# A hybrid recurrence block: TensorE's instructions in the order of emission instead of the scheduler's, in the part with the recurrences

## The chip, the cores and the metric

One Trainium2 chip, one of its cores. The kernel is one program with one launch. The metric is the time of one execution on the device in microseconds (us), as a median over runs; lower is better. TensorE (PE in the rows) multiplies matrices out of on-chip memory into PSUM, VectorE (DVE), ScalarE (ACT) and GpSimd (POOL) do the elementwise work, and SyncE (SP) issues most transfers. Each engine takes its instructions strictly one after the other, and an instruction waits on semaphores until what it reads has been written.

## The reference, cut to what matters

One layer on 256 latent and 256 context tokens with 2048 channels. A modulated norm is followed by one wide projection; its columns feed two recurrent branches (RWKV-7 and a gated delta rule, each in two directions, the latent scan starting from the context's last state) and two merge gates. Then up-projections, gates, an output projection, a residual, and a squared-ReLU MLP with a second residual and a last norm.

```python
    p = h @ in_w
    pc = hc @ (in_w[:, :A_COLS + B_COLS] if last else in_w)
    ...
    ya, ya_c = rwkv7_branch(pa.astype(f32), pca.astype(f32), ...)
    yb, yb_c = gdn_branch(pb.astype(f32), pcb.astype(f32), ...)

    x = x + g1 * merge_branches(ya.astype(dt), yb.astype(dt), pg, up_a, up_b, out_w)
    x = x + g2 * squared_relu_mlp(modulate(rms_norm(x, norm2_w), sh2, sc2), mlp_w1, mlp_w2)
```

All is float32. A dense product is made of three matmuls on operands split into a high and a low part (`mm3`, lines 239 to 241), which run in the type float32r; the recurrences use plain float32 matmuls.

## The kernel before, in words

The time falls into four stretches. To about 180 us the modulation and the first projections are made. From there to about 1455 us runs the part with the recurrences, which this change is about. Then come the merge and the output projection (to about 1800 us) and the MLP.

In the part with the recurrences four kinds of work are woven together. The **dense** work is projections (`projg`): 16 steps over the k tiles, three matmuls a step, of 256 or 512 columns, into a PSUM tile `dacc` of which there are two. Three **lanes** run beside it, each a Python generator: `preps` prepares a pair of heads (eight pairs), `invs` inverts the triangular 32 x 32 blocks of a pair, and `chains` walks through the chunks of a pair. When the RWKV pairs are through, the same lanes do the gated delta rule (`gpreps`, `ginvs`, `gchains`), with the merge's gates and up-projections as dense work.

`weave` sets the order in which all of this is emitted. Every `yield` of the dense generator says how long TensorE is busy with the step; every `yield` of a lane says how much dense time is to pass before the lane's next step. So the distance between two dependent steps of a lane is written by hand, in units of dense work. Where a generator emits two dependent things with no `yield` between them, they are emitted side by side.

The order of emission isn't the order on the engines: a scheduler sorts each engine's instructions when the program is built. It takes emission order as a priority, but puts an instruction later where, by its own reckoning, its inputs are not there yet, and takes others in between. From then on each engine's order is fixed.

The places that the prediction speaks of:

- `l2n` and `conv_silu` (lines 590 to 610): a head's q or k columns are convolved, gated and normalised. After the last matmul of the projection come ScalarE (591), VectorE (595, 596), ScalarE (598), VectorE (599) and ScalarE (603); then TensorE multiplies the squares by a matrix of ones (604). No `yield` stands between. Eight of these have 256 columns (q), eight 512 (k). In `prep` (line 647) the same is done for RWKV's k, behind six operations of VectorE (437) and two of ScalarE (434, 646), eight times, seven of them in this part.
- `tri_inv` (lines 465 to 482): one VectorE transpose (469), then 31 times two dependent VectorE operations (478, 480), then a transpose back (481). TensorE's line 811 (RWKV) or 1146 (delta rule) reads the result. The blocks that are inverted come from TensorE's lines 741 and 744 (RWKV) or 1079 (delta rule). There are eight inversions for RWKV and four for the delta rule, and the lane lets dense work pass at nine places in each.
- `wgran` (line 217): a weight tile is brought in by SyncE and split by ScalarE (226) and VectorE (227), with the highest priority.
- `gemv_steps` (line 279): the modulation's rows, fp32 matmuls of 512 columns (289), now and then between dense steps; a copy of the sums (294), then small matmuls on the copy (300, 309).

Of the kernel before, what the change touches and what calls it, by code (L numbers as in the profile page):

```python
# [131 lines left out]
def body(tc, A, out, dbg=None):  # L132
# [33 lines left out]
    class First:  # L166
        """An engine whose instructions go ahead of the others that are ready."""
# [12 lines left out]
    def weave(dense, lanes):  # L180
        """Emits dense, whose steps say how long the tensor engine is at them, and between its steps those of the lanes, which
        say how long to let pass before the next one. lanes: (generator, stretch)."""
        t, at = 0.0, [[g, 0.0, f] for g, f in lanes]

        def step(a):
            try:
                a[1] = max(a[1], t - 1) + next(a[0]) * a[2]
            except StopIteration:
                at.remove(a)

        slot = 0
        for c in dense:
            t += c
            if t < slot:
                continue
            slot = t + Q
            for a in list(at):
                while a in at and a[1] <= t + Q / 2:
                    step(a)
        while at:  # L200
            for a in list(at):
                step(a)

    nraw, more = 0, None  # the room that a phase adds to the ring of weights: a pool's tag, and how many of its tiles
# [9 lines left out]
    def wgran(src):  # L214
        """Half a megabyte of weights [128, K, C]: for each half of K (hi, lo), in tiles of their own."""
        K, w = src.shape[1], src.shape[2]
        raw = rawt()
        nc.sync.dma_start(out=raw[:, :K * w].rearrange("p (k c) -> p k c", k=K), in_=src)
        F = K // 2 * w
        r = []  # L220
        for i in range(2):
            hi = stream.tile([128, 512], F32R, tag="hi", name="hi")
            lo = stream.tile([128, 512], F32R, tag="lo", name="lo")
            x = raw[:, i * F:(i + 1) * F]
            with tc.high_priority(1000000):
                S.copy(out=hi[:, :F], in_=x)  # L226
                V.tensor_tensor(out=lo[:, :F], in0=x, in1=hi[:, :F].bitcast(F32), op=ALU.subtract)  # L227
            r.append((hi, lo))
        return r

    def wk_(g, k, w):
        """The (hi, lo) columns of k tile k, w wide, out of a granule of eight (w = 128) or two (w = 512) k tiles."""
        n = 512 // 128 if w != 512 else 1
        hi, lo = g[k // n]
        c = slice(k % n * w, k % n * w + w)
        return hi[:, c], lo[:, c]
# [26 lines left out]
    # modulation per channel: columns (x, ctx) for chunk tiles  # L263
# [15 lines left out]
    def gemv_steps(n, pool, acc, ahead=0):  # L279
        """Row n of the modulation, one half-megabyte of weights a step; at last the sums as four groups of rows."""  # L280
# [35 lines left out]
    # the same room once the projections are through: yb (0:8), the merged halves (8:24), ya (24:32), then half the MLP  # L316
# [18 lines left out]
    with ExitStack() as st:  # L335
        p0 = st.enter_context(tc.tile_pool(name="p0", bufs=2, reuse_waits="tile"))
        psg = st.enter_context(tc.tile_pool(name="psg0", bufs=1, space=PSUM))
        # x / sqrt(mean(x^2) + eps)
# [16 lines left out]
        def part(j):  # L355
            """The projections of first over the k tiles 4 j to 4 j + 3."""
# [73 lines left out]
    # z' = z + (shift(z) - z) mu ; natural order [ctx | x]  # L430
# [21 lines left out]
    def fl(ap, d, n=512):  # L452
        """[P, n] in scan order of direction d."""
# [8 lines left out]
    def tri_inv(pool, dg, xt):  # L462
        """X = (I - L)^-1 of the strictly upper 32 x 32 blocks L = dg[32 q:32 q + 32, u, :32], sixteen in each group of 32
        partitions: blocks to lanes (two lanes a block, one for the even rows of X and one for the odd ones), then row by
        row of L. Writes X^T to xt, in the places of dg."""
# [18 lines left out]
    def gate(j, tile_):  # L484
        """tanh of half the gate columns j of the merge, to DRAM."""
# [19 lines left out]
    def dense(every, *gens):  # L505
        """The steps of gens, and after each so many of them one of the modulation's."""
# [9 lines left out]
    with ExitStack() as st:  # L516
# [12 lines left out]
        def decays():  # L529
            """The decay and beta of the delta rule, token-major [tok, tile, (dir, head)]."""  # L530
# [124 lines left out]
        def prep2(p, R):  # L655
            zk, zv, zr, kk = (R[n] for n in ("zk", "zv", "zr", "kk"))
            # lora weights of this pair
# [8 lines left out]
            for d in range(2):  # L666
                # decay
# [8 lines left out]
                # the products up to a token (inclusive) or before it (exclusive), in the direction's order  # L676
# [14 lines left out]
                # in-context rate  # L691
# [27 lines left out]
                # bonus  # L719
# [5 lines left out]
                # pairwise products inside a chunk  # L725
# [40 lines left out]
                # token-major beta, kappa  # L766
# [12 lines left out]
            # the bonus  # L779
# [7 lines left out]
        def inv2(p, R):  # L787
            """The inverses of the chunks: a comes before b."""
# [40 lines left out]
            # values by tokens, in the rows beside their head's state  # L829
# [10 lines left out]
        ORD = ((0, 1, 2, 3, 4, 5, 6, 7), (3, 2, 1, 0, 7, 6, 5, 4))  # the chunks in the order in which a direction goes through them  # L840
        VL = S1.copy

        def chain(p, R):
            vt = R["vt"]

            def vload(d, sgm):
                """[S | U] beside V for two chunks; head 0 has V in the upper rows, head 1 in the lower ones."""
# [74 lines left out]
            # readout  # L922
# [40 lines left out]
        def rgates():  # L963
            """The gates of RWKV for all pairs."""
# [51 lines left out]
        GL = []  # the decays; the masks of a tile's pairs  # L1016
# [9 lines left out]
        NAT = ((0, 1, 2, 3), (1, 0, 3, 2))  # the tiles in the order in which a direction goes through them  # L1026
# [6 lines left out]
        def ltile(h, d):  # L1033
            """Room for the pairwise products of a head and direction, for three heads in turn."""
# [11 lines left out]
        def gprep(hh, hi_, R):  # L1046
            """Both directions in the tokens' own order: what comes first lies above the diagonal or below it."""
# [61 lines left out]
        def ginv(R, begun, wait):  # L1109
            """The inverses of 128 tokens out of those of 32, both directions at once: r0 comes before r1."""  # L1110
# [163 lines left out]
        gated, spilt = [], []  # the heads of yb that were done before the last product out of hT  # L1274
# [25 lines left out]
        def room():  # L1300
            """What is left of the inverses' room goes to the ring of weights."""
# [25 lines left out]
        def works():  # L1327
            nonlocal every
            yield from work()
            every = 12  # L1330
            yield from gwork()

        mpool = gpp
        weave(dense(lambda: every, works()),
# [7 lines left out]
    with ExitStack() as st:  # L1342
# [44 lines left out]
        def gate2():  # L1387
            """The second gate, in every partition."""
# [20 lines left out]
        def tokmm(src, kts, acts, n, done):  # L1409
            """out[tok, 512 columns n] over k tiles kts; acts[k] the [k, tok] pair."""  # L1410
# [18 lines left out]
        def resid(i, n, ps, c):  # L1429
            """x += gate * ps for the columns n; with c, the sum of their squares to column c."""  # L1430
# [15 lines left out]
        # x1 by channels, scaled but for its norm; beside it the shift, whose product with w1 is added after the norm  # L1446
# [90 lines left out]
```

## Time and profile before

| | before |
|---|---|
| median of 3 runs | 2349.41 us (2346.86 to 2351.87) |
| profiled execution, first to last instruction | 2348.0 us |
| TensorE matmuls busy | 2252.8 us |
| TensorE weight loads busy | 1795.2 us |
| VectorE busy | 1584.3 us |
| ScalarE busy | 1349.2 us |

The profiled execution has no time of its own beside its span; the span lies 1.4 us under the median of the runs. Matmuls are pipelined and overlap in the records, so the busy time of TensorE has to be read together with how many matmuls start in a stretch.

### The profile page before, as it was taken

The numbers are of one execution on the slowest core, as the hardware profiler recorded it, in microseconds if no ns is written. First come the engines' busy times: TensorE is split into PE (matmuls) and PEld (weight loads), VectorE is DVE, ScalarE is ACT, GpSimd is POOL, SyncE is SP. The second block draws the span as 40 slices with busy tenths as digits, with TensorE's granted clock in tenths as the row PEclk, the third lists the DMA queues.
The fourth block names the chain that finished last, engine by engine and source line by source line (L and its number), as shares of the span: only waits on it lengthen the run. The fifth ranks groups of instructions, "written<-read, shape, count | busy, mean of one in ns | idle before, by whom it ended". The sixth has DMA issues, their size and how long they took to land.

```text
span 2348.0 us, 45265 instructions
## 1 busy us (share of the span) xinstructions
PE 2252.8 (96%) x16886; PEld 1795.2 (76%) x16886; DVE 1584.3 (67%) x3590; ACT 1349.2 (57%) x3003; POOL 158.4 (7%) x343
## 2 busy tenths in 40 slices
PE   6989999999999999999999999999999999999997
PEld 2557676766667676678787888878999888999886
DVE  2357885858686867668577786876887555666555
ACT  3235758475758575855565766456555444555544
POOL 0001021111111111111000000000000000000000
PEclk9999999999999999999999999999999999999999
DMA  9954333333333343457566554875776666555664
GB/s 363 311 166 136 109 109 103 131 106 120 108 118 118 120 125 108 147 174 234 180 215 217 188 159 138 292 255 181 251 259 216 194 192 196 181 181 182 193 193 149
DMA packets 184371, 417.94 MB, mean 178 GB/s; under 512 B 15380, under 2 KB 37076, under 8 KB 183128
## 3 DMA queue, kind: packets, MB, share of 16 engines
q1 hardware_dynamic: 183576, 414.02, 55.1%
q8 instruction: 132, 2.16, 0.4%
q10 hardware_dynamic: 576, 1.05, 0.1%
q14 instruction: 87, 0.71, 0.1%
HBM read 399.63 MB, written 15.38 MB: 177 GB/s over the span
## 4 chain that ended last, share of the span: by engine, by line
PE 65%; ACT 6%; DVE 3%; DMA 2%; issue 1%; SPq 0%; ACTq 0%; DVEq 0%
PE dacc L239 12%; PE dacc L241 11%; PE dacc L240 11%; PE dacc L1423 3%; PE pm L1422 3%; PE pm L1421 3%; PE pm L1423 3%; PE dacc L1422 3%; PE dacc L1421 3%; PE vacc L289 3%; ACT hi L226 1%; DMA raw<-in_mod_w_dram 1%; DVE lo L227 1%; DMA raw<-in_w_pg_dram 1%; PE cb L889 1%
## 5 line engine op out<-in xcount | busy, mean ns | idle before, releaser
L227 DVE TENSOR_TENSOR lo<-raw,hi 128x512 fp32r<-128x512 f32 (+1 forms) x1032 | 693.0, 677 | 456.4 <-ACT hi L226 272.7
L226 ACT CAST hi<-raw 128x512 fp32r<-128x512 f32 (+1 forms) x1032 | 625.7, 610 | 646.1 <-PE dacc L240 315.4
L239 PE MATMUL dacc<-hh,hi 128*128 128x256 f32 (+1 forms) x1648 | 562.4, 342 | 8.5 <-ACT hh L244 3.5
L241 PE MATMUL dacc<-hh,lo 128*128 128x256 f32 (+1 forms) x1648 | 531.0, 322 | 1.3 <-DVE lo L227 1.2
L240 PE MATMUL dacc<-hl,hi 128*128 128x256 f32 (+1 forms) x1648 | 530.5, 322 | 0.0
L239 PEld LDWEIGHTS dacc<-hh,hi 128*128 128x128 f32 x1648 | 313.8, 191 | 98.9 <-issue 56.0
L241 PEld LDWEIGHTS dacc<-hh,lo 128*128 128x128 f32 x1648 | 314.1, 191 | 26.2 <-issue 3.5
L240 PEld LDWEIGHTS dacc<-hl,hi 128*128 128x128 f32 x1648 | 314.8, 191 | 23.5 <-issue 7.0
L241 PE MATMUL dacc<-ah,lo 128*128 128x258 f32 x1024 | 291.7, 285 | 1.7 <-DVE lo L227 1.6
L239 PE MATMUL dacc<-ah,hi 128*128 128x258 f32 x1024 | 290.8, 284 | 1.1 <-ACT ah L244 1.1
L240 PE MATMUL dacc<-al,hi 128*128 128x258 f32 x1024 | 290.1, 283 | 0.0
L241 PEld LDWEIGHTS dacc<-ah,lo 128*128 128x128 f32 x1024 | 194.2, 190 | 4.1 <-DVE lo L227 3.0
L239 PEld LDWEIGHTS dacc<-ah,hi 128*128 128x128 f32 x1024 | 194.6, 190 | 2.4 <-ACT ah L244 1.3
L240 PEld LDWEIGHTS dacc<-al,hi 128*128 128x128 f32 x1024 | 194.3, 190 | 1.1 <-issue 1.0
L175 POOL TENSOR_SCALAR sp<-vu,pc 64x64 f32<-64x64 f32 x224 | 128.2, 572 | 408.9 <-DVE vu L175 357.0
L1423 PE MATMUL dacc<-lo,hh 128*128 128x512 f32 x320 | 125.8, 393 | 4.0 <-DVE lo L227 3.8
L1421 PE MATMUL dacc<-hi,hh 128*128 128x512 f32 x320 | 125.0, 391 | 0.3 <-ACT hi L226 0.3
L1421 PE MATMUL pm<-hi,hh 128*128 128x512 f32 x320 | 124.8, 390 | 0.0
L1422 PE MATMUL dacc<-hi,hl 128*128 128x512 f32 x320 | 124.8, 390 | 0.0
L1423 PE MATMUL pm<-lo,hh 128*128 128x512 f32 x320 | 124.6, 389 | 0.0
L1422 PE MATMUL pm<-hi,hl 128*128 128x512 f32 x320 | 124.6, 389 | 0.0
L289 PE MATMUL vacc<-raw,sc_st 128*32 128x512 f32 x384 | 113.5, 605 | 1.6 <-DMA raw<-in_mod_w_dram 1.6
(411 smaller groups left out, 3255.9 us busy)
## 6 DMA issues: line engine op xcount, KB each, us to landing
raw<-in_w_dram SPq DMA_DIRECT2D x256, 512.0 KB
raw<-in_mod_w_dram SPq DMA_DIRECT2D x192, 512.0 KB
raw<-in_w_gdn_dram SPq DMA_DIRECT2D x64, 512.0 KB
raw<-in_w_pg_dram SPq DMA_DIRECT2D x64, 512.0 KB
raw<-in_w_rkv_dram SPq DMA_DIRECT2D x40, 512.0 KB
raw<-in_out_w_dram SPq DMA_DIRECT2D x32, 512.0 KB
raw<-in_upa_dram SPq DMA_DIRECT2D x16, 512.0 KB
raw<-in_upb_dram SPq DMA_DIRECT2D x16, 512.0 KB
```

The source lines that it names most:

```text
L175: return getattr(self.eng, name)(*a, **k)
L226: S.copy(out=hi[:, :F], in_=x)
L227: V.tensor_tensor(out=lo[:, :F], in0=x, in1=hi[:, :F].bitcast(F32), op=ALU.subtract)
L239: P.matmul(out=o, lhsT=wh, rhs=ah, start=first, stop=False)
L240: P.matmul(out=o, lhsT=wh, rhs=al, start=False, stop=False)
L241: P.matmul(out=o, lhsT=wl, rhs=ah, start=False, stop=last)
L289: P.matmul(out=pm[32 * g:32 * g + 32, :], lhsT=sc_st[:, 2 * k:2 * k + 32], rhs=raw[:, r * 512:(r + 1) * 512], start=(k < 4), stop=(k >= 12 ...
L889: P.matmul(out=cbs[d][hr[h], 64:128], lhsT=R["ti"][hr[h], d * 8 + ns[d], :], rhs=rss[d][hr[h], :], start=True, stop=True)
L1421: P.matmul(out=pss[i], lhsT=ah[:, tsl], rhs=wh, start=first, stop=False)
L1422: P.matmul(out=pss[i], lhsT=al[:, tsl], rhs=wh, start=False, stop=False)
L1423: P.matmul(out=pss[i], lhsT=ah[:, tsl], rhs=wl, start=False, stop=last)
```

## The change

The call of `weave` for the part with the recurrences now stands inside a region that orders TensorE: there each TensorE instruction is issued in the order in which the kernel emits it. The order on the other engines, and where the region's instructions fall among those emitted outside it, stay the scheduler's. Nothing is added, removed or computed in another way; comments and descriptive strings were dropped, and lines behind the change carry a number higher by one.

```diff
         mpool = gpp
-        weave(dense(lambda: every, works()),
+        with tc.manual_schedule(engines={mybir.EngineType.PE}):
+            weave(dense(lambda: every, works()),
               [(both(chains(), stretch(F_GC / F_C, gchains())), F_C), (both(invs(), ginvs()), F_I),
                (both(preps(), stretch(F_GP / F_P, gpreps())), F_P)])
         for _ in md:
             pass
```

**First place: TensorE at the norm of a head's q** (second pair of heads). `dacc` is the PSUM tile of a projection, `hh` and `hl` are the split activations by k tile (hh_102 is the first k tile, hh_132 the last), `hi` and `lo` the split weights, `gth` the squares. Before, the row of line 604 stands in the middle of the next projection, which has 512 columns; its own projection, of 256 columns, ended 34 rows earlier:

```order
L239 MATMUL dacc<-hh_114,hi 128x512
L240 MATMUL dacc<-hl_115,hi 128x512
L241 MATMUL dacc<-hh_114,lo 128x512
L239 MATMUL dacc<-hh_116,hi 128x512
L240 MATMUL dacc<-hl_117,hi 128x512
L241 MATMUL dacc<-hh_116,lo 128x512
L239 MATMUL dacc<-hh_118,hi 128x512
L604 MATMUL dacc<-gth,cs 128x256
L240 MATMUL dacc<-hl_119,hi 128x512
```

In the changed kernel, TensorE at the same place:

```order
L239 MATMUL dacc<-hh_130,hi 128x256
L240 MATMUL dacc<-hl_131,hi 128x256
L241 MATMUL dacc<-hh_130,lo 128x256
L239 MATMUL dacc<-hh_132,hi 128x256
L240 MATMUL dacc<-hl_133,hi 128x256
L241 MATMUL dacc<-hh_132,lo 128x256
L604 MATMUL dacc<-gth,cs 128x256
L239 MATMUL dacc<-hh_102,hi 128x512
L240 MATMUL dacc<-hl_103,hi 128x512
```

Line 604 moved up to the row directly behind the last matmul of its own projection, and the whole next projection now stands behind it.

**Second place: TensorE at an inversion** (fifth pair of heads). `pr` is the PSUM tile of the inversion, `ti` and `X` hold the inverses that VectorE makes, `off` the other blocks; `cb` belongs to the chain of the pair before. Before, 90 dense matmuls of 256 columns and 69 of 512 stand between the last row of line 741 and the first of line 811, whose surroundings are:

```order
L912 MATMUL cb<-mb,vu 64x64 x2
L239 MATMUL dacc<-hh_110,hi 128x512
L240 MATMUL dacc<-hl_111,hi 128x512
L241 MATMUL dacc<-hh_110,lo 128x512
L239 MATMUL dacc<-hh_112,hi 128x512
L240 MATMUL dacc<-hl_113,hi 128x512
L241 MATMUL dacc<-hh_112,lo 128x512
L239 MATMUL dacc<-hh_114,hi 128x512
L240 MATMUL dacc<-hl_115,hi 128x512
L241 MATMUL dacc<-hh_114,lo 128x512
L811 MATMUL pr<-ti,off 32x32
L239 MATMUL dacc<-hh_116,hi 128x512
```

In the changed kernel 42 of 256 and 42 of 512 columns stand between them:

```order
L871 MATMUL cb<-vu,eb 64x64 x4
L239 MATMUL dacc<-hh_126,hi 128x512
L240 MATMUL dacc<-hl_127,hi 128x512
L241 MATMUL dacc<-hh_126,lo 128x512
L239 MATMUL dacc<-hh_128,hi 128x512
L240 MATMUL dacc<-hl_129,hi 128x512
L241 MATMUL dacc<-hh_128,lo 128x512
L811 MATMUL pr<-ti,off 32x32
L811 MATMUL pr<-X,off 32x32
L811 MATMUL pr<-ti,off 32x32
L811 MATMUL pr<-X,off 32x32
```

Line 811 moved up past 75 dense matmuls, and all 32 of its rows now stand together.

**Third place: VectorE inside the same inversion.** `Lt` and `ltmp` are the inversion's, `lo` a weight split, `vu` the chain's state, `zr` a projection's result. Before:

```order
L469 STREAM_TRANSPOSE Lt<-dg 128x32x32
L478 TENSOR_TENSOR ltmp<-X,Lt 128x31
L227 TENSOR_TENSOR lo<-raw,hi 128x512
L175 SCALAR_TENSOR_TENSOR vu<-cb,pc,sp 64x64 x4
L783 TENSOR_TENSOR bs<-pg,zv 128x256
L480 TENSOR_TENSOR X<-X,ltmp 128x31
L478 TENSOR_TENSOR ltmp<-X,Lt 128x30
L480 TENSOR_TENSOR X<-X,ltmp 128x30
L478 TENSOR_TENSOR ltmp<-X,Lt 128x58
L227 TENSOR_TENSOR lo<-raw,hi 128x512
```

In the changed kernel:

```order
L469 STREAM_TRANSPOSE Lt<-dg 128x32x32
L478 TENSOR_TENSOR ltmp<-X,Lt 128x31
L480 TENSOR_TENSOR X<-X,ltmp 128x31
L478 TENSOR_TENSOR ltmp<-X,Lt 128x30
L480 TENSOR_TENSOR X<-X,ltmp 128x30
L478 TENSOR_TENSOR ltmp<-X,Lt 128x58
L480 TENSOR_TENSOR X<-X,ltmp 128x2x29
L478 TENSOR_TENSOR ltmp<-X,Lt 128x56
L480 TENSOR_TENSOR X<-X,ltmp 128x2x28
L478 TENSOR_TENSOR ltmp<-X,Lt 128x81
```

VectorE's other instructions moved out of the beginning of the inversion. Between lines 469 and 481 of this inversion stand 38 other instructions before and 18 in the changed kernel.

## Rows read from the trace of the kernel before

**Rows 1.** The page's first line.

```profile
span 2348.0 us, 45265 instructions
```

**Rows 2.** Busy time of each engine by stretch: start:end, length, busy us (instructions), clock, DMA.

```profile
180.00:1455.00 1275.00, 1235.98 (x10740) 931.46 (x10739) 921.35 (x2379) 828.74 (x1987) 157.10 (x332) 0.99 0.46 143
2050.00:2100.00 50.00, 50.00 (x417) 50.00 (x416) 32.33 (x60) 28.17 (x61) 0.00 (x0) 1.00 0.58 186
1850.00:1900.00 50.00, 50.00 (x223) 41.39 (x222) 27.46 (x41) 23.38 (x38) 0.00 (x0) 1.00 0.63 194
```

**Rows 3.** TensorE's waits, 180 to 1455 us: total us, times, longest.

```profile
PE dacc L604 <- ACT gth L603: 5.3, 5, 2.7
PE pr L811 <- DVE ti L481: 3.6, 4, 1.2
```

**Rows 4.** Timeline of one norm of 256 columns: start us, us, engine, line.

```profile
365.36 0.46 ACT L591 ACTIVATE qv<-dacc,vs 128x256 f32<-128x256 f32 x1
...
366.27 0.48 DVE L595 SCALAR_TENSOR_TENSOR qv<-dacc,vs,qv 128x255 f32<-128x255 f32 x1
...
367.00 0.47 DVE L596 SCALAR_TENSOR_TENSOR qv<-dacc,vs,qv 128x255 f32<-128x255 f32 x1
...
367.57 0.42 ACT L598 ACTIVATE gth<-qv 128x256 f32<-128x256 f32 x1 [0.23 <-DVE qv L596]
...
369.22 0.42 DVE L599 SCALAR_TENSOR_TENSOR qv<-gth,qv 128x256 f32<-128x256 f32 x1
...
369.67 0.42 ACT L603 ACTIVATE gth<-qv 128x256 f32<-128x256 f32 x1
...
370.14 0.48 PE L604 MATMUL dacc<-gth,cs 128*128 128x256 f32 x1 [0.26 <-ACT gth L603]
```

**Rows 5.** Timeline of one norm of 512 columns, first and last step.

```profile
493.75 0.67 ACT L591 ACTIVATE kv<-dacc,vs 128x512 f32<-128x512 f32 x1
...
499.60 1.22 PE L604 MATMUL dacc<-gth,cs 128*128 128x512 f32 x1 [2.70 <-ACT gth L603]
```

**Rows 6.** VectorE's inversion groups, 180 to 1455 us: busy us, mean ns | idle before.

```profile
L478 DVE TENSOR_TENSOR ltmp<-X,Lt 128x126 f32<-128x126 f32 (+22 forms) x372 | 94.1, 253 | 7.3
L480 DVE TENSOR_TENSOR X<-X,ltmp 128x126 f32<-128x126 f32 (+22 forms) x372 | 93.9, 252 | 8.1
```

**Rows 7.** Timeline of the fifth inversion: its input, first and last steps, and reader.

```profile
652.44 1.16 PE L741 MATMUL pg<-eb,bk 64*128 64x128 f32 x16
...
659.42 1.99 DVE L469 STREAM_TRANSPOSE Lt<-dg 128x1024 f32<-128x1024 f32 x1
...
699.01 1.11 DVE L481 STREAM_TRANSPOSE ti<-X 128x512 f32<-128x512 f32 x1
...
700.54 0.24 PE L811 MATMUL pr<-ti,off 32*32 32x32 f32 x2
```

**Rows 8.** Groups of VectorE's other work, 180 to 1455 us.

```profile
L227 DVE TENSOR_TENSOR lo<-raw,hi 128x512 fp32r<-128x512 f32 x372 | 253.9, 688 | 150.5 <-ACT hi L226 131.0 <-PE dacc L239 5.3 <-PE dacc L241 4.3
...
L175 DVE SCALAR_TENSOR_TENSOR vu<-cb,pc,sp 64x64 f32<-64x64 f32 x224 | 59.9, 282 | 32.9 <-PE cb L905 19.7 <-PE cb L912 6.1 <-POOL vu L175 1.6
```

**Rows 9.** A small matmul and the copy of the modulation's sums, 180 to 1455 us.

```profile
L889 PE MATMUL cb<-rs,ti 64*64 64x64 f32 x512 | 30.6, 231 | 0.8 <-ACT rs L175 0.6
...
L294 ACT COPY rows<-vacc 128x512 f32<-128x512 f32 x12 | 7.1, 589 | 8.1 <-PE vacc L289 8.1
```

**Rows 10.** Busy time by stretch behind one stop of TensorE, and around another.

```profile
175.00:180.00 5.00, 5.00 (x20) 3.73 (x21) 2.70 (x8) 3.28 (x5) 0.00 (x0) 0.64 0.00 0
...
1380.00:1385.00 5.00, 1.92 (x12) 1.54 (x12) 4.64 (x13) 3.48 (x7) 0.00 (x0) 0.85 0.50 172
1385.00:1390.00 5.00, 4.38 (x20) 4.38 (x21) 3.73 (x13) 1.35 (x3) 0.00 (x0) 0.50 0.54 158
```

**Rows 11.** Timeline of TensorE where dense work follows a small matmul.

```profile
1350.30 0.36 PE L240 MATMUL dacc<-hl,hi 128*128 128x256 f32 x1
1350.50 0.28 PE L241 MATMUL dacc<-hh,lo 128*128 128x256 f32 x1
```

## The prediction

> **What bounds the kernel now.** I read the stretches first. The part with the recurrences takes 1275 us of the span of 2348.0 [rows 1, 2], and in it some TensorE matmul is open for 1236 us. The first thing to see is that nearly nothing else could end this stretch: VectorE is busy 921 us, ScalarE 829. The second is how fast dense work goes when nothing is in its way: in the MLP 417 matmuls of 258 columns start in 50 us, 0.120 us each, and 223 of 512 columns, 0.224 us each [rows 2]. These two prices I use for all dense work that covers a wait. The third is the list of TensorE's waits: its longest entries in this part are only 5.3 us (line 604) and 3.6 us (line 811) in total [rows 3]. So before the change the results that come back from VectorE and ScalarE are hidden almost wholly, and the question is what hides them in the new order.
>
> **What the change does, place by place.** It adds and removes nothing. It fixes where TensorE must stand still until a result arrives. In the order before, such rows stand late enough; in the new one each stands where it was emitted. For every row of TensorE that reads another engine's result I compare the work that TensorE has between the result's own source and that row (the cover) with the time that the result needs.
>
> Chain steps of RWKV (lines 871, 889, 905) keep what they had: the lane's yields leave some 2 to 5 us of TensorE's work between two steps in either order. They cost nothing new, and neither do lines 741 and 771, whose covers hardly change.
>
> *1. The norms, lines 604 and 647.* In the new order line 604 stands directly behind the last matmul of the projection that it normalises. What must happen in between is six dependent steps. For 256 columns they last 0.46 + 0.48 + 0.47 + 0.42 + 0.42 + 0.42 = 2.7 us, and in the instance shown 4.8 us passed from the first step to the matmul, since other work lay between them on both engines [rows 4]. I take the middle, 3.7 us: TensorE stands, so less new work arrives, but weight splits go first. For 512 columns the same took 5.85 us [rows 5]; a wider operation isn't faster, so 2.7 is the lower end, and I take 5.0, near the row. Line 647 has eight steps of 512 columns or half of it, and I give it 5.0 too. Eight of the first kind, seven of the second (the eighth lies inside an inversion), and four of line 647 (three others stand behind an inversion's stop, which hides them): 8 x 3.7 + 11 x 5.0 = 85 us (51 to 103).
>
> *2. RWKV's inversions, line 811.* The result needs 1.99 + 31 x (0.253 + 0.252) + 1.11 = 18.8 us of VectorE alone [rows 6, 7], and before it 5.8 us from the end of line 741 (652.44 + 1.16) to the start of line 469 [rows 7]. In the new order VectorE has 18 to 26 other instructions inside the inversion (11 in the first pair), 22 on the mean, from 0.282 to 0.688 us each [rows 8]; at 0.45 that is 10 us. Together 34.6 us. The cover in the new order of the fifth pair is 42 x 0.120 + 42 x 0.224 = 14.4 us of dense work; the mean over the second to the seventh pair is 13.4. To this come 40 chain matmuls at 0.12 us (30.6 us over 256, each of which has two records) [rows 9], 4.8 us, and some 20 others, for which I take 4.2. So 22.4 us, and a stop of 12.2 us, seven times. The first pair has only 10.8 + 4 us of cover against 29.6, 14.8 us. Sum 100 us. The bounds: with no other work on VectorE 24.6 − 22.4 = 2.2 us each and 9.8 for the first pair, 25 us in all; with VectorE as slow as before, when line 811 came 46.9 us behind line 741 [rows 7], 24.5 us each, 196 us. I stand between, since the new order of VectorE has about half as much other work inside an inversion, not none.
>
> *3. The delta rule's inversions, line 1146.* The four covers lose 264 matmuls of 256 columns together, 32 us at 0.120; VectorE's order has 42 fewer other instructions inside, 19 us at 0.45. The stop lies between 13 and 32 us in all; bounded below by 0 if the waits before were slack. I take 20.
>
> *4. Small stops.* The modulation's copies (589 ns, [rows 9]) stand directly ahead of their readers twelve times; some 20 further places (the second half of line 834, the one-time gates and decays, the first pair) are alike. 32 x 0.6 = 19 us (7 to 32).
>
> *5. What comes back.* Dense work and small matmuls alternate 1094 times in the old order and 936 times in the new one. A dense matmul of 256 columns behind a small one is followed after 0.20 us, not after 0.12 [rows 2, 11]; 158 x 0.08 = 13 us. The waits of [rows 3], 9 us, are part of the span and are replaced by the new ones. Minus 22 us.
>
> *6. The clock.* After a stop of some microseconds the rows show TensorE at its lower level, 1.2 GHz, for a part of the next stretch: a granted clock of 0.64 from 175 to 180 us, 1.8 us lost, and 0.50 from 1385 to 1390 us behind a stop, 2.5 us lost [rows 10]. The eleven long stops of points 2 and 3 at 2.2 us make 24 us (0 to 28). The Trainium skill's page "TensorE: Matmul & The Clock Gate" (section "HAM oscillation — how this bites in real kernels") tells of a kernel that fell back to the lower clock at each of its repeated waits; by that the short stops of point 1 would pay as well. No row here shows a stop of that length with its clock, so this is left to the upper rival.
>
> Sum: 85 + 100 + 20 + 19 − 22 + 24 = 226 us on the profiled 2348.0, so 2574; the median lies 1.4 us above the span, so I forecast **2575 us**, slower by some 9 to 10%. A change of 0.2% is about what a measurement of this kernel can tell from none.
>
> **The rivals.**
>
> *Only the norms stop.* VectorE, with TensorE standing still at the norms, may be ahead when an inversion begins, and point 2 falls to its lower bound, 25 us, point 3 to nothing, the clock to 5. For it: VectorE is idle for a good quarter of the stretch (921 of 1275 us [rows 2]). Against it: none of the norms stands inside the first seven inversions in the new order, and 18.8 us of dependent steps leave 3.6 us. 85 + 25 + 19 − 22 + 5 = 112 us: 2461.
>
> *VectorE stays as slow as before, and every stop costs clock.* Point 2 rises to 196 us, and the 19 short stops of point 1 pay the clock as the long ones do, 19 x 2.2 = 42 us: 226 + 96 + 42 = 364 us: 2713. For it: the weight splits (0.688 us [rows 8]) go ahead of everything. Against it: the third place of the new order, where ten rows of the inversion stand without a stranger.
>
> *Not slower: the emission order is good enough.* One mechanism: the hand-set distances cover the results, and what remains is point 5, minus 22 us: 2327. It decides where the cover exceeds the result's time; behind line 604 that cover is nothing. For it speaks that the chain's steps are covered in both orders, and that weight loads, another measure, are open for 931 of 1275 us only [rows 2]. The Trainium skill's page "Trainium Kernel Development and Optimization" (section "Performance Expectations") calls matmul busy time a bad metric and weight-load time a good one; by it a quarter of the stretch is slack. Against it: slack on TensorE is of use only where the order lets other work in, and the new order lets none in.
>
> **How the numbers follow.** My forecast 0.62; only the norms 0.16; the slow VectorE 0.17; not slower 0.05 (faster 0.04, the same 0.01). The forecast's own range is 2500 to 2650. To hold 8 in 10 the whole range goes to 2440 at the lower end (into the first rival) and 2700 at the upper (into the second): 0.05 and about half of each of the two lie outside, near 0.2. Chances: faster 0.04, the same 0.01, slower 0.95.
>
> **What would show it.** Point 1: line 604 waits for line 603 sixteen times, 3 to 6 us each, most of 90 us in the list of waits. Point 2: line 811 waits for line 481 eight times, about 12 us each. Point 3: line 1146 the same, about 5 us each. Point 5: the other waits of the stretch stay small, and the MLP keeps its pace. Point 6: some ten stretches with a granted clock under 1.0 between 250 and 1500 us. The prediction is wrong if line 811 waits less than 4 us, if ScalarE holds up the chain's steps (waits of 889 or 905 of tens of microseconds, which I priced at nothing), or if VectorE delays the dense work's own weight splits.

## The result, and the profile after

The changed kernel takes 2650.86 us (median of 4 runs, 2648.47 to 2661.13) against 2350.64 us of the kernel before in the same session (4 runs, 2346.86 to 2355.24): a ratio of 1.1274, with a 95% interval of 1.125 to 1.130. The forecast was 2575 us with a range of 2440 to 2700; the time lies inside it, 76 us above the forecast and just above the forecast's own part of it (2500 to 2650).

The page's first lines and the stretches of the changed kernel, which answer to [rows 1, 2]:

```profile
span 2648.4 us, 45317 instructions
...
PE 2300.6 (87%) x16886; PEld 1836.2 (69%) x16886; DVE 1602.9 (61%) x3590; ACT 1360.3 (51%) x3003; POOL 153.4 (6%) x343
```

```profile
180.00:1755.00 1575.00, 1281.86 (x10755) 971.24 (x10755) 940.80 (x2382) 837.62 (x1986) 152.08 (x332) 0.90 0.37 116
2350.00:2400.00 50.00, 50.00 (x417) 50.00 (x416) 32.34 (x61) 28.01 (x61) 0.00 (x0) 1.00 0.56 185
2150.00:2200.00 50.00, 50.00 (x222) 41.38 (x222) 27.12 (x40) 23.01 (x37) 0.00 (x0) 1.00 0.60 195
```

The part with the recurrences, some 10,750 matmuls as before, takes 1575 us instead of 1275: all 300 us lie there, and the MLP keeps its pace (417 and 222 matmuls in 50 us, against 417 and 223). The granted clock of that part is 0.90 instead of 0.99. VectorE and ScalarE did the same work in more time; neither became the bound of the stretch as a whole (940.8 and 837.6 of 1575 us).

TensorE's waits in that stretch (line, what ended the wait, us in total, times, longest), which answer to [rows 3]:

```profile
PE dacc L604 <- ACT gth L603: 80.8, 16, 7.8
PE pr L811 <- DVE ti L481: 74.5, 7, 13.7
PE pr L1146 <- DVE xt L481: 22.0, 3, 11.3
PE dacc L647 <- ACT t L646: 18.3, 4, 5.0
PE pg L771 <- DVE mb L758: 14.3, 16, 1.9
PE pg L565 <- issue: 8.9, 1, 8.9
PE pr L834 <- ACT vt L836: 8.8, 8, 2.9
PE pg L744 <- DVE bk L703: 7.6, 1, 7.6
PE vacc L300 <- ACT rows L294: 7.3, 8, 2.5
PE pr L980 <- DVE sg L970: 5.9, 1, 5.9
PE cb L1200 <- ACT gs L175: 4.8, 5, 2.5
PE cb L1223 <- ACT vn L175: 4.3, 4, 1.5
PE pr L811 <- DVE X L798: 3.5, 7, 0.5
```

Over the whole span all lines of this list sum to 333.8 us after and 81.0 us before, 252.8 us more. TensorE's busy time, for the same 16886 records, grew by 47.8 us (2300.6 − 2252.8). Together they are 300.6 us, and the span grew by 300.4: nothing else is left to explain. The ledger by terms of the prediction (waits after minus waits before, from the two lists):

| term | forecast | measured |
|---|---|---|
| 1: lines 604 and 647 | 85 | 80.8 + 18.3 = 99 |
| 2: line 811 | 100 | 74.5 + 3.5 = 78 |
| 3: line 1146 | 20 | 23 |
| 4: all other waits, after minus before | 19 | 133.3 − 70.2 = 63 |
| 5: old waits of these four lines that went | −9 | −11 |
| 5 and 6: alternations and clock, as busy time | −13 + 24 = 11 | 48 |
| sum | 226 | 300 |

The clock is read from the reader itself. These are TensorE's instructions at the fourth 512-column norm of the changed kernel (start, us, line; in brackets the idle time before):

```profile
737.30 2.07 PE L604 MATMUL dacc<-gth,cs 128*128 128x512 f32 x2 [7.33 <-ACT gth L603]
738.39 1.42 PE L239 MATMUL dacc<-hh,hi 128*128 128x512 f32 x1
```

and the two stretches of 5 us around it, which answer to [rows 10]:

```profile
735.00:740.00 5.00, 2.70 (x4) 1.50 (x5) 4.86 (x11) 3.22 (x5) 0.23 (x2) 0.50 0.02 5
740.00:745.00 5.00, 5.00 (x22) 3.54 (x21) 0.69 (x1) 3.68 (x8) 0.00 (x0) 0.67 0.13 52
```

In the stretch in which the reader starts, the granted clock is 0.50, that is 1.2 GHz; TensorE comes back to 2.4 GHz within the next one. All eight 512-column readers of line 604 lasted 1.22 us in their first record, against 0.59 or 0.70 us in the kernel fill_norms below, and six of the eight 256-column ones 0.80 instead of 0.48 us, behind idle times of 3.6 to 7.8 us.

### The profile page after: what moved, and what is told of

Its sections match the earlier page's. It is cut to its first block, busy times and chain, and to the rows that moved or that the text cites. A ratio compares the mean times of both kernels' runs of the same rounds, so it can differ in the third digit from the quotient of the medians.

```text
span 2648.4 us, 45317 instructions
## 1 busy us (share of the span) xinstructions
PE 2300.6 (87%) x16886; PEld 1836.2 (69%) x16886; DVE 1602.9 (61%) x3590; ACT 1360.3 (51%) x3003; POOL 153.4 (6%) x343
## 4 chain that ended last, share of the span: by engine, by line
PE 45%; DVE 4%; ACT 3%; DMA 3%; issue 1%; SPq 0%; ACTq 0%; DVEq 0%
PE dacc L239 8%; PE dacc L240 7%; PE dacc L241 7%; PE dacc L1424 3%; PE pm L1422 3%; PE pm L1423 3%; PE pm L1424 3%; PE dacc L1423 3%; PE dacc L1422 3%; PE vacc L289 1%; DMA raw<-in_w_pg_dram 1%; DVE lo L227 1%; ACT hi L226 1%; DMA raw<-in_mod_w_dram 1%; PE cb L1209 0%
## 5 line engine op out<-in xcount | busy, mean ns | idle before, releaser
L239 PE MATMUL dacc<-hh,hi 128*128 128x256 f32 (+1 forms) x1648 | 608.6, 369 | 5.4 <-ACT hh L244 4.4
L240 PE MATMUL dacc<-hl,hi 128*128 128x256 f32 (+1 forms) x1648 | 538.6, 327 | 0.6 <-DVE hl L245 0.4
L239 PEld LDWEIGHTS dacc<-hh,hi 128*128 128x128 f32 x1648 | 329.2, 200 | 95.5 <-issue 52.5
L240 PEld LDWEIGHTS dacc<-hl,hi 128*128 128x128 f32 x1648 | 330.7, 201 | 29.2 <-issue 12.1
L241 PEld LDWEIGHTS dacc<-hh,lo 128*128 128x128 f32 x1648 | 328.4, 199 | 23.7 <-DVE lo L227 0.4
L289 PE MATMUL vacc<-raw,sc_st 128*32 128x512 f32 x384 | 103.8, 620 | 0.0
```

What stands on the lines that cost most here:

```text
L239: P.matmul(out=o, lhsT=wh, rhs=ah, start=first, stop=False)
L240: P.matmul(out=o, lhsT=wh, rhs=al, start=False, stop=False)
L241: P.matmul(out=o, lhsT=wl, rhs=ah, start=False, stop=last)
L289: P.matmul(out=pm[32 * g:32 * g + 32, :], lhsT=sc_st[:, 2 * k:2 * k + 32], rhs=raw[:, r * 512:(r + 1) * 512], start=(k < 4), stop=(k >= 12 ...
```

## The experiments

All are edits of the changed kernel; three of them (those named scheduler) also take the change itself back. "Wait" is the sum of TensorE's list of waits, "busy" TensorE's busy time; before they were 81.0 and 2252.8 us, in the changed kernel 333.8 and 2300.6.

**norms: the norms' readers emitted later.** `l2n` and `prep` now return what follows the squares, and the next projection calls it after some steps:

```diff
-            P.matmul(out=q[:, :n], lhsT=C("ones"), rhs=sq[:, :n], start=True, stop=True)
+            def rest():
+                P.matmul(out=q[:, :n], lhsT=C("ones"), rhs=sq[:, :n], start=True, stop=True)
...
-            ps = yield from projg(A["w_gdn"][8 + h], 128, False)
+            ps = yield from later(projg(A["w_gdn"][8 + h], 128, False), 8, rest)
```

> The changed kernel, but the product of lines 604 and 647 and what follows it of the norm are emitted 8 (13 for line 647) matmul groups later, inside the next projection. TensorE still issues in order of emission. Theory (the time lies in the stops at the results' readers): the waits of 604 and 647, 81 and 18 us in the changed kernel's list of waits, go; so does the half-clock stretch behind each. 2651 - 99 - about 25 of clock = about 2525 us. Rival (VectorE and ScalarE have become the bound, and the stop at 604 only stands where their backlog shows): the time reappears at the next readers, lines 771, 811 and 834, and the kernel stays above 2620 us.

Measured 2542.02 us (2540.91 to 2544.03), ratio 1.081 (1.079 to 1.083). Line 604 is line 606 in this kernel, 811 is 829, 771 is 789, 834 is 852:

```profile
PE pr L829 <- DVE ti L481: 77.5, 8, 13.7
PE pr L1164 <- DVE xt L481: 22.3, 3, 11.3
...
PE pg L789 <- DVE mb L776: 14.3, 15, 1.9
PE dacc L606 <- ACT gth L603: 10.6, 8, 2.2
...
PE pr L852 <- ACT vt L854: 7.3, 8, 1.3
```

Of the norms' 99 us of waits 10.6 are left, and about 8 us came back elsewhere, most of them at line 741 (759 here: 8.4 us instead of 1.1): waits 253.7 us (80 fewer), busy 2270.6 (30 fewer), 109 us in the time, 17 less than the theory said. The 30 us are the same matmuls running faster, 1.5 us for each of 20 stops. The theory holds, and the rival (above 2620 us) falls.

**fill_norms: TensorE kept busy in the norms' waits.** Extra matmuls into a free tile, which nothing reads:

```diff
             S.activation(out=sq[:, :n], in_=dst[:, :n], func=AF.Square)
+            qf = pr()
+            for _ in range(8 if n == 256 else 12):
+                P.matmul(out=qf[:, 0:256], lhsT=C("ones"), rhs=cs[:, 0:256], start=True, stop=True)
```

> The changed kernel with extra fp32 matmuls of 256 columns into a free PSUM tile ahead of line 604: 8 (about 3.4 us) in its eight 256-column cases and 12 (about 5.2 us) in its eight 512-column cases, where TensorE waited 4.0 and 6.0 us on the mean. TensorE is busy for most of those waits, and waits for the same results afterwards; the work added is about 69 us, the wait that it stands in 81 us. Theory (each of these short stops also costs half-clock time behind it, as the 30 us of busy time say that came off when the 19 norms' stops were taken away): the time falls, by 16 x 1.5 = 24 us, to about 2627 us. Rival (the 30 us came off for another reason, the clock costs nothing here): no change, 2645 to 2660 us, or more if the filler outlasts a wait.

Measured 2630.42 us (2627.18 to 2634.22), ratio 1.118 (1.116 to 1.120): 20 us faster than the changed kernel, with more work in it, and 3 us from the theory's 2627. The reader of the same norm as above is line 607 here, the filler line 606 (its row begins where the view does, with 22 of the 24 records):

```profile
721.65 4.91 PE L606 MATMUL pr<-cs 128*128 128x256 f32 x22
728.71 1.34 PE L607 MATMUL dacc<-gth,cs 128*128 128x512 f32 x2 [2.15 <-ACT gth L603]
729.27 1.20 PE L239 MATMUL dacc<-hh,hi 128*128 128x512 f32 x1
```

Its two records last 1.34 us instead of 2.07. None of the 16 readers runs at the lower clock any more. The sixteen fillers, from first start to last end, stand open for 72.0 us, but busy time grew by 41.4 only (2342.0 − 2300.6): the other matmuls took 30.6 us less, 1.9 us a stop. That is the 30 us of the kernel norms, by another way. So the short stops pay the clock.

**fill: the same ahead of the inversions' reader,** 22 matmuls ahead of line 811 and 8 ahead of line 604's 256-column case, there into columns 256 to 511 of the tile that the norm reads.

> The changed kernel with 22 extra fp32 matmuls of 256 columns (about 9.4 us) into unused columns ahead of line 811, eight times, and 8 of them (about 3.4 us) ahead of the 256-column case of line 604, eight times: TensorE is busy in the time in which it would wait, and waits for the same result afterwards. Nothing that the kernel needs is changed. It tells the clock's share from the wait's. Theory (TensorE falls to half clock behind these stops, and that costs about 2 us each): the time falls although work is added, by 15 to 30 us, to about 2625 us, and there are some 15 fewer stretches of granted clock under 1. Rival (the half clock costs nothing, since the matmuls there wait for something else): no change, 2645 to 2660 us.

Measured 2672.30 us (2671.95 to 2673.57), ratio 1.136 (1.135 to 1.138): 21 us slower, and outside both expectations. The rows say why (605 is the filler at the norms, 606 the norm's reader, 815 is 811):

```profile
PE dacc L606 <- ACT gth L603: 48.4, 8, 7.8
...
PE dacc L605 <- DVE qv L596: 21.9, 8, 3.8
...
PE pr L815 <- DVE ti L481: 9.6, 4, 4.3
```

The norms' filler was badly placed: it waits for line 596, which reads the tile that it writes, 2.7 us a time, and then keeps TensorE for 39.8 us in all, since five of the eight fillers run wholly or partly at the lower clock; where the readers had waited 32 us, wait and filler now take 62. What the run still shows: all fillers stand open for 39.8 + 77.4 = 117.2 us, busy grew by 93.7, so the other matmuls took 23.5 us less. How much of that belongs to the long stops this run can't divide. The changed kernel has seven of them at line 811; if the norms' fillers slowed nothing else, it is at most 3.4 us each.

**invs: more dense work inside the inversions,** `yield 2.6` for `yield 1.5` in `tri_inv` (both places).

> The changed kernel, but the eight places inside an inversion at which the emission gives way to dense work ask for 2.6 instead of 1.5 units of it, so that more dense work lies between an inversion's start and its reader, lines 811 and 1146. Theory: the waits of 811 (75 us) and 1146 (22 us) go, with some 10 to 20 us of clock; but the chains and preparations, which get the less dense work, stop no more than before: 2651 - 97 - 15 = about 2540 us. Rival (VectorE is the bound inside the inversions): with more dense work emitted there, more weight splits lie in VectorE's queue ahead of the rows of the inversion, the wait moves and stays above half, and the kernel stays above 2600 us.

Measured 2590.55 us (2587.5 to 2595.3), ratio 1.101 (1.099 to 1.103): 60 us of the 111 expected, between the two expectations.

```profile
PE dacc L604 <- ACT gth L603: 79.9, 16, 8.8
PE dacc L647 <- ACT t L646: 37.0, 7, 5.6
...
PE pr L811 <- DVE ti L481: 7.9, 1, 7.9
...
PE pr L1146 <- DVE xt L481: 2.2, 1, 2.2
```

The waits of 811 and 1146 went, 91 us by the lists. But three of line 647's stops, which had stood behind an inversion's stop and cost nothing, now wait 16 us (its whole entry is 19 us larger), and short ones came up at lines 239 and 1243 (waits 276.9 us, 57 fewer). Some of the inversions are now hidden by such stops instead of by work. So a fixed order pays the longer of two stops that lie one behind the other, and taking one away uncovers the next. Busy time stayed at 2302.7 us though eight of the ten long stops went: the 10 to 20 us of clock that the theory promised did not come, and this run can't tell whether the long stops cost little or the new ones took their place.

**dose: less dense work there,** `yield 0.5` for `yield 1.5`.

> The changed kernel, but the eight places inside an inversion at which the emission gives way to dense work ask for 0.5 units of it instead of 1.5: the work between line 741 and line 811 falls from about 22 to 15 us, that between line 1079 and line 1146 from about 35 to 24 us. Theory (the stop is result time less cover, and VectorE's own time doesn't shrink with it): each of the twelve waits grows by most of the cover lost, 8 x 6 + 4 x 9 = about 85 us, less what comes back because the weight splits that went with that dense work leave VectorE's queue (20 to 40 us): 811 and 1146 wait 140 to 180 us together instead of 100, and the kernel takes about 2700 us. Rival (VectorE is slow inside the inversions because of the splits, so fewer of them make it faster by as much): 811 and 1146 as before, 2640 to 2660 us.

Measured 2727.71 us (2726.03 to 2728.24), ratio 1.159 (1.157 to 1.161).

```profile
PE pr L811 <- DVE ti L481: 104.9, 7, 17.8
PE dacc L604 <- ACT gth L603: 90.4, 16, 7.8
PE pr L1146 <- DVE xt L481: 45.2, 4, 18.5
PE dacc L647 <- ACT t L646: 34.7, 7, 5.6
```

Lines 811 and 1146 wait 155 us with their small second entries (3.5 and 1.6), 54 more than in the changed kernel. In the second to the seventh RWKV pair the matmuls between lines 741 and 811 fall from 23 to 14 us, but the stop grows by only half of that (from 10.8 to 15.2 us), since VectorE also has fewer weight splits inside an inversion (three instead of five). The theory's interval for these waits holds; the time is 28 us above its estimate, 16 of it at line 647 and 10 at line 604.

**both: the two edits at once.** The modulation's steps also wait now while a norm is open, since its rows and the norm's use the same room.

> Both edits at once, in order of emission. Theory: the two effects add, since the stops are in different places: 2651 - 99 - 97 - about 25 to 40 of clock = about 2420 us, and the rest above the kernel before (2351) are the small stops of some tens of microseconds. Rival (the dense work is a fixed stock: what covers the one is missing at the other): clearly less than the sum of the two, above 2480 us.

Measured 2529.91 us (2528.14 to 2534.38), ratio 1.076 (1.074 to 1.078). 121 us, not 109 + 60, with the held modulation in it as a third edit. The matmuls of line 239 (a third of the dense work) near the end of the recurrences, with the clock behind the counts:

```profile
1575.00:1600.00 25.00, 10.07 (x35) 6.56 (x35) 0.93 0.42 126
1600.00:1625.00 25.00, 0.54 (x1) 0.33 (x1) 0.57 0.02 6
1625.00:1650.00 25.00, 6.25 (x18) 4.48 (x17) 0.75 0.31 98
```

For some 30 us there is hardly any dense work left, and the last chains run one small matmul behind the other at a clock of 0.57. The larger distances were paid out of a fixed stock. Line 811 (839 here) also waits 37 us again, against 8 in invs: VectorE has eight weight splits inside an inversion here and five in invs, with the same 2.6 units. That TensorE's stops at the norms held the splits back there is a guess that no run tests.

**both_scheduler, norms_scheduler, balanced_scheduler: three emissions under the scheduler's order,** by taking the one line of the change back:

```diff
-        with tc.manual_schedule(engines={mybir.EngineType.PE}):
+        if True:
             weave(dense(lambda: every, works()),
```

> The emission of the kernel both (2530 us in its own order), but TensorE in the scheduler's order, as in the kernel before. Theory (the scheduler already puts other work in front of a reader whose result is late): the edits of the emission are worth nothing under it, 2340 to 2365 us. Rival (part of what the edits bought lies in the emission itself, as more room for the scheduler): faster than before by over 0.5%, below 2338 us.

Measured 2403.89 us (2403.31 to 2412.34), ratio 1.0225 (1.020 to 1.025): slower than before, against both. Up to 1300 us it is only 98 of 10,007 matmul records behind the kernel before, some 12 us. Most of the rest is in one place (line 239 again):

```profile
1425.00:1450.00 25.00, 14.34 (x47) 9.75 (x48) 0.93 0.57 173
1450.00:1475.00 25.00, 3.68 (x13) 2.41 (x13) 0.64 0.18 56
1475.00:1500.00 25.00, 1.12 (x2) 0.67 (x2) 0.64 0.02 5
```

The same bare end. The scheduler hides stops, but it can't make dense work that has been used up.

> The emission of the kernel norms in the scheduler's order. In the kernel both_scheduler (2404 us) the dense work was missing from 1450 to 1510 us, as in the same emission's own order; with the inversions' 1.5 units the recurrences do not outlast the dense work. Theory (the 52 us were that bare end alone): 2345 to 2360 us, as the kernel before. Rival (moving the norms away from their projections hurts the scheduler by itself): above 2375 us.

Measured 2356.17 us (2351.59 to 2360.51, 10 runs), ratio 1.0008 (0.9995 to 1.002). An edit that is worth 109 us in the fixed order is worth nothing under the scheduler.

> The emission of the kernel balanced (2516 us in its own order; RWKV's inversions with 2.6 units, its chain steps with 1.2) in the scheduler's order. Theory (under the scheduler only the end counts: whether dense work is left when the recurrences end): as the kernel before, 2340 to 2360 us, though the inversions have the same 2.6 units that stand in both_scheduler (2404 us). Rival (the 2.6 units themselves cost the scheduler its room): above 2375 us.

Measured 2395.97 us (2391.23 to 2408.04), ratio 1.019 (1.015 to 1.022). The theory falls: dense work lasts to 1550 us here and TensorE's waits are 92 us, little more than before, yet busy time grew by 31 us at nearly the same clock (0.988 against 0.992), and at 1100 us the trace is already 263 of 8162 records behind. Dense and small matmuls alternate 1242 times in this trace and 1182 times before, which points the way but is too little at 0.08 us. The rival's time holds (above 2375 us), but what makes the 2.6 units cost it stays open.

**balanced (the emission of balanced_scheduler, in its own order): norms moved, 2.6 units in RWKV's inversions only, RWKV's chain steps cut.**

```diff
-CW, F_C, F_P, Q, GW, F_GP, GCW, F_GC, NG, MR, Y = 1.5, 1.5, 0.9, 0.0, 1.65, 0.9, 1.2, 0.6, 2, 16, (2, 2.5, 2, 2, 0, 1)
+CW, F_C, F_P, Q, GW, F_GP, GCW, F_GC, NG, MR, Y = 1.2, 1.5, 0.9, 0.0, 1.65, 0.9, 1.2, 0.6, 2, 16, (2, 2.5, 2, 2, 0, 1)
```

> The norms moved as in the kernel norms (2542 us), RWKV's inversions alone with 2.6 units (the delta rule's keep 1.5), and the chain's steps of RWKV with 1.2 units instead of 1.5, so that the recurrences don't outlast the dense work at the end. Theory (what the two edits lost together, 2530 us instead of about 2480, is dense work that was missing at the end of the delta rule): the waits of 811 go down to some 10 us, the bare stretch at the end does not come, and the kernel takes about 2480 us. Rival (the dense work is short everywhere, so that the chain's steps, with a fifth less, begin to wait: lines 889, 905, 871): the waits move there, 2520 to 2560 us.

Measured 2516.07 us (2508.97 to 2520.93), ratio 1.069 (1.067 to 1.072), between the two. The bare end didn't come, busy time fell to 2257.7, nearly that of before. But line 811 (829 here) still waits 45 us: VectorE has some 30 other instructions inside an inversion, nine of them weight splits, against 18 to 26 with five splits in the changed kernel and three splits in dose. More cover brought more weight splits here, and they lengthen what it is to cover; in invs alone it did not (five).

**small_stops: the kernel norms, with more distance at lines 771 and 834** (`Y[1]` 4 for 2.5, a `yield 2` between the halves of 834), and with the modulation's steps held as in both.

> The kernel norms (2542 us) with two more edits in order of emission: 4 units of dense work instead of 2.5 behind each group of pairwise products (ahead of line 771's transposes, whose waits are 14 us), and 2 units between the two halves of line 834's transposes (7 us). Theory (small stops are stops too, at about 1 us each with half a microsecond to a microsecond of clock): some 18 us of wait go and 10 to 20 us of pace come back, about 2510 us. Rival (stops under 2 us cost no clock, and the dense work is only moved to where it is missing next, the inversions): 2525 to 2545 us.

Measured 2542.28 us (2539.45 to 2545.94), ratio 1.080 (1.078 to 1.083): the same as norms, as the rival said. Line 771 (799 here) fell from 14.3 to 4.8 us, but the held steps of the modulation came in groups:

```profile
PE vacc L309 <- ACT rows L294: 11.6, 4, 4.8
PE vacc L300 <- ACT rows L294: 10.4, 8, 4.4
...
PE pg L799 <- DVE mb L786: 4.8, 5, 1.8
```

Waits are 250.0 us against 253.7. What one place won another lost; since the modulation was held too, the run doesn't test the two distances alone.

**best_order: all that seemed to pay** (RWKV's inversions 3.2, chain steps 1.0, `Y[1]` 3.5, 834's halves, norms moved, the modulation's steps held).

> All edits that seemed to pay, in order of emission: norms moved, RWKV's inversions with 3.2 units, the small stops' distances (3.5 units, and 2 between the halves), and RWKV's chain steps with 1.0 instead of 1.5 so that the recurrences end while dense work is left. Theory (only the stops matter, and dense work that the chain does not need can cover them): the waits of line 811 fall from 42 us in the kernel balanced to under 15, and the kernel takes about 2470 us; the kernel before is not reached, since the delta rule's 17 to 25 us, the one-time stops (744, 565, 980) and many waits of 1 us stay. Rival (a fixed order with as much slack per reader needs more dense work than there is): the chain's lines take over what 811 loses, 2500 to 2530 us.

Measured 2498.93 us (2492.59 to 2505.24), ratio 1.062 (1.059 to 1.065): just at the edge of the rival's interval; but the chain's lines hardly took over what 811 lost. TensorE waits 143 times, 219.9 us in all, the largest line 811 with 42, 27 us at the modulation's lines 300 and 309; busy is 2257.6. Half of the loss is won back, and the rest is spread over many readers.

## Why the prediction was right, and where its size was off

**What bounds the kernel, and the mechanism.** Right. The work is the same, and TensorE's stops at late results are the loss, 253 of 300 us by the list of waits. That both edits of the emission won time back in the fixed order, and norms_scheduler none (1.0008), shows it: it was the lost freedom to put other work ahead of a late reader. The size came out too low by 74 us of the span, term by term +14, −22, +3, +44, −2 and +37: points 4 and 6 were priced far too low, and point 2 makes up for a part of it.

**Point 1, the norms: 99 us for 85.** Line 604 waits sixteen times as forecast, on the mean 4.05 us for 256 columns (3.7 assumed) and 6.05 for 512 (5.0 assumed). For 256 columns the middle was the right choice; for 512 the instance of [rows 5], 5.85 us, would have been.

**Point 2, RWKV's inversions: 78 us for 100.** The result's time, with the most guesses in it, came out best: line 811 comes 34.5 us behind line 741 in the fifth pair (34.6 forecast) and 32.7 to 37.6 in the second to seventh, 35.5 on the mean, with 18 to 26 other instructions on VectorE. The cover was taken too small: 35.5 less these six stops' mean of 10.8 is 24.7, not 22.4, and 1.3 of it are other stops of TensorE. That makes 9 us of the 22, and the first pair (9.9 for 14.8) 5 us. The largest part is the eighth pair, whose 12.2 us were counted in full and did not come (line 811's small second entries give 3.5 us back):

```profile
1234.65 1.22 PE L604 MATMUL dacc<-gth,cs 128*128 128x512 f32 x1 [5.46 <-ACT gth L603]
1254.30 0.60 PE L565 MATMUL pg<-gl,c 128*128 128x32 f32 x2 [8.93 <-issue]
1278.96 0.21 PE L811 MATMUL pr<-ti,off 32*32 32x32 f32 x1
```

These stops of TensorE lie inside that inversion (16.8 us with the smaller ones), and the inverse (line 481) was there 18 us before line 811. The prediction had seen a norm inside it and dropped the norm's stop; it is the inversion's stop that went. In norms, where that norm no longer stops there, line 811 waits eight times. That the cover's matmuls last longer at a lower clock, and so hide more, would explain the rest, but was not tested. The lower bound, and with it the rival "only the norms stop", would have needed a VectorE without other work. The rival "VectorE stays as slow as before" (24.5 us each) is refuted by the same 34.5 us.

**Point 3: 23 for 20.** Right in the sum; three stops of 3.8 to 11.3 us make it, not four of about 5, so that the sum agrees is in part luck.

**Point 4, small stops: 63 us for 19.** This failed. The modulation's copies cost 10 us and line 834 7, as the list of places said, at more than 0.6 us each. But the prediction said that lines 741 and 771 "cost nothing new": 771 waits sixteen times, 14.3 us against 2.6. The row before:

```profile
PE pg L771 <- DVE mb L758: 2.6, 5, 1.2
```

The one-time places (565, 744, 980) were each taken as 0.6 us and cost 5.9 to 8.9. And the delta rule's chains (1200, 1209, 1223, 1234) wait 13 us against 3: only RWKV's chain steps were checked, and these are indeed not in the list.

**Points 5 and 6, alternations and clock: 48 us for 11.** The forecast had the clock at 2.2 us for the long stops alone, eleven by its count (there were ten). norms and fill_norms give 1.5 and 1.9 us for the short ones: 20 of them make 30 to 38 us. If the alternations brought their 13 us, some 23 to 31 us are left for the long stops and the small ones. No run measured these apart: fill allows at most about 3.4 us for a long one, and in invs eight of them went without any fall of the busy time. That part of the upper rival (the short stops of point 1 pay the clock, 42 us) was right though its other part was not. The sign for this point, some ten stretches with a granted clock under 1.0, was far exceeded: 93 of the 250 stretches of 5 us between 250 and 1500 us show one, against 7 before. The step that failed is a reading: "No row here shows a stop of that length with its clock". [rows 5] does: its reader lasts 1.22 us behind a stop of 2.70 us, and the other seven of 512 columns in that trace last 0.59 or 0.70. So does [rows 10]: the stretch at 0.50 comes behind two stops of two microseconds, in the trace before:

```profile
1381.72 0.50 PE L239 MATMUL dacc<-hh,hi 128*128 128x256 f32 x2 [1.90 <-ACT hh L244]
1385.62 0.58 PE L239 MATMUL dacc<-hh,hi 128*128 128x256 f32 x1 [1.99 <-DVE gu L1264]
```

I read the rows for their idle time and not for the duration behind it. The Trainium skill's page "TensorE: Matmul & The Clock Gate" (section "HAM oscillation — how this bites in real kernels") tells of a fall at each of a kernel's repeated waits; this trace agrees at 14 of line 604's 16.

**Not slower.** The weight loads' open time, by which a quarter of the stretch was slack, said nothing of the order: the slack was there after the change too (971 us of 1575) and no instruction could use it. The Trainium skill's page "Trainium Kernel Development and Optimization" (section "Performance Expectations") calls weight-load time a good metric for how close a kernel is to roofline; in this trace its share of the stretch fell with the change, from 73% to 62%, and it could not tell beforehand which results an order hides.

## What to carry to other kernels

Where an engine's order is fixed by hand, every reader that stands next to its source becomes a stop; list these readers, also the one-time ones, and price each at the result's time less the cover, plus the clock, here 1.5 to 1.9 us behind a stop of 3.6 to 7.8 us (for longer and shorter ones no run here has the price). Two stops that lie one behind the other cost only the longer. Cover is a stock: what one reader is given is missing elsewhere or at the end, so more distance helps only as far as dense work is left and as long as it does not feed the engine that is waited for. The duration of the instruction behind a stop, against the same instruction elsewhere, shows TensorE's clock where a window is too coarse.

## What was unexpected of the hardware

Work that nothing reads made the kernel faster: 72 us of filler ahead of line 604 took 20 us off the time, because the stops turned from idle to busy and the 16 readers behind them, and what followed, ran at 2.4 GHz (0.48 and 0.59 to 0.70 us instead of 0.80 and 1.22). Two 256-column readers of the changed kernel kept 0.48 us behind idle times of 3.64 and 3.77 us, while others fell to 0.80 behind 3.61 and 3.77, so the length of the stop alone does not tell the level.
